# When plain jobs split their weights, and how much selection runs beside the recurrence, in a fp32 hybrid block on one Trainium2 core

## The chip, the cores and the metric

The kernel runs on one core of a Trainium2 chip. The engines are named as the profile names them: PE (TensorE, matrix products; PEld is its loading of the stationary operand), DVE (VectorE), ACT (ScalarE), POOL (GpSimd) and SP (SyncE, here only the queue that starts the transfers). The metric is the device time of one execution in microseconds (us).

## What is computed

The reference is one layer of a streaming block over 512 tokens of width 2048, all in fp32. After an RMS norm, one wide projection gives the inputs of two mixers. Branch A is a gated linear recurrence with 8 heads of 128 (here called the recurrence). Branch B is attention in which a small indexer with 16 heads scores all visible keys and each query keeps its 128 best (here called the selection). Both are gated, projected, merged and projected back.

```python
h = rmsnorm(x, norm_w)
(a_q, a_f, a_i, a_g, c_q, c_kv, k_idx, w_idx, b_g, m_a, m_b) = split(h @ w_in)
q, f, v = silu(a_q) / sqrt(128), lb + (1 - lb) * sigmoid(a_f), a_i
state = exp(sum log f) * state + decayed(1 - f).T @ v      # per chunk of 64
y_a = rmsnorm(q * decay @ state + causal(q, 1 - f) @ v) * silu(a_g)
score = sum_h relu(q_idx[h] @ k_idx.T) * w_idx[h]           # 16 heads
top_val, top_idx = top_k(score, 128)                        # the selection
y_b = softmax(q @ k[top_idx] + t5_bias) @ v[top_idx] * silu(b_g)
x = x + (sigmoid(m_a) * (y_a @ w_pa) + sigmoid(m_b) * (y_b @ w_pb)) @ w_out
return rmsnorm(x, final_norm_w)
```

## The kernel before, in words

Each fp32 product is made of three products of rounded halves: an operand is split into a high part (`wh`, a rounded copy made by ACT, line 90) and a low part (`wl`, the difference, made by DVE, line 91), and `mm3` issues high*high, high*low and low*high (lines 94, 95, 96).

The program is a list of jobs, run in order; each engine works through its own queue in the order in which the program was written. **Plain jobs** are `feat_job` (a tile of features by 512 tokens; the names `cq`, `kx`, `hf`, `hq`, `aq` are its outputs), `ai_job` (the recurrence's values) and `ukv_job`. A plain job takes its weights in chunks of 1024 numbers per partition (512 for the one-tile job of `kx`). **Pair jobs** take 7 products in place of 8 on blocks, with their own preparation in `pair_unit`; the change leaves them as they are.

The way of a chunk: `load` (line 147, queue of SP) fetches it into one of two buffers `wr`; the split reads `wr` and writes one of three pairs `wh`/`wl`; PE reads them. `prep(i)` issues the splits up to chunk i+2, and `load_ahead` the loads for up to two chunks beyond the last one split. A load has to wait until the low part of the chunk two before it has been taken from the same buffer.

Beside the jobs run **lanes**: generators that each do one step whenever a job calls `pump()`, in the order hgrn, top, att, norm, misc, t5. A plain job pumps twice or so in a chunk: `ai_job` after every second of its four k-blocks, a job with two tiles after each tile, the one-tile job after the chunk. The lane `hgrn` (`hgrn_gen`) does the recurrence of two heads in 8 levels. At a level, PE makes a burst of small products (`hl<-hq,hk`, line 99), and then DVE multiplies decay factors into `hq` and `hk` (lines 785, 792, 794; `tot`, line 803, is the running factor), and copies what the level masks (`hnear`, line 816). The next burst reads the new `hq` and `hk`; after the last level PE transposes `hk` (`hkt`, line 834). The lane `norm` has, in the same stretch, products of a vector with a row (`nt`, line 604) that ACT rounds (`ckh`, line 605). The lane `misc` has `pair_gen`: per step sums of x (`sv`, lines 1080 to 1087) and their split (`s`).

The lane `top` (`top_gen`) does the selection: 3 blocks of 16 iterations, each a `MAX8` and a `MATCH_REPLACE8` over the scores `M` (lines 684, 685), and at a block's end one line 687. It paces itself: at each pump its credit grows by 2.7 minus `R.load`, a number that `hgrn_gen` sets at each of its steps, and each iteration costs 0.4 + 0.27(b+1). When the job `uqkv(0)` begins (the first queries of the attention), `drain("top")` issues what is left of the selection at once.

Near the end stands **the merge**: eight jobs of two tiles and two chunks that multiply by `w_pb`. `pb_evac` empties each tile's sum times its gate (`mg<-acc,mg`, line 1365) and adds the other mixer's (line 1366). Behind the second tile a generator `merge_pair` joins the lane `misc`. At the next pumps it takes differences of the two tiles on DVE (`hv`, lines 1339 to 1342) and rounds the tiles on ACT (`mh` and `m21h`, lines 1343 to 1345); then it takes the low parts on DVE (`ml` and `m21l`, lines 1348 to 1350) and rounds and splits the sums (`so`, lines 1347 and 1354). One pump later `m21h` and `m21l` are stored to DRAM (`m_d`, line 1352, queue of SP). There is one buffer for `m21h` and one for `m21l`, so that the rounding for the next two tiles waits until the store has landed. In SP's queue the store stands behind the loads of two chunks, and ahead of the loads of the next gates (line 1300). The output job (`pp`), a pair job, follows; its chunks are split by `prep` as well (lines 164 to 173: `sv`, `bh`, `bl`, `wh`, `wl`), and the first of them within the last of the eight jobs.

The order of the jobs around the change: `cq` in two halves with `kx` between them, `ckv`, the pair jobs of the gates, eight jobs for the indexer, then ai(3) and ai(2), f and q of pair 0, ai(1), f and q of pair 1, `uqkv(0)`, a gate job, and the rest of the attention and of the merge. Beside them run the recurrences of the pairs 3, 2, 0 and 1, in this order.

Of the kernel before, what the change touches and what calls it, by code (L numbers as in the profile page):

```python
# [68 lines left out]
def hybrid_block(ctx, tc, x, norm_w, w_in, lb_table, gnorm_a, q_norm_w, kv_norm_w, w_uq,  # L69
# [19 lines left out]
    def split(hi, lo, src):  # L89
        A.activation(hi, src, AF.Copy)  # L90
        V.tensor_tensor(lo, src, hi.bitcast(F32), op=OP.subtract)  # L91
# [43 lines left out]
    R = SimpleNamespace(load=0.0)  # L135
# [3 lines left out]
    raws, halves = {}, {}  # L139
# [10 lines left out]
    def load_ahead():  # L150
        while issued[0] < min(issued[1] + 2, len(specs)):
            load(issued[0])
            issued[0] += 1

    def weight_places(at):
        return [wpool.tile([128, WCAP + 64], FR, name=name)[:, at:at + WCAP] for name in ("wh", "wl")]
# [19 lines left out]
    def prep(i):  # L176
        while issued[1] < min(i + 3, len(specs)):
            j = issued[1]
            if specs[j][3:4] == ("pair",) and not hasattr(R, "g"):
                if j > i + 1 and lanes["norm"]:  # L180
                    break
                open_pairs()
            load_ahead()
            _, kc, n = specs[j][:3]
            t = raws.pop(j)
            if specs[j][3:4] == ("pair",):
                halves[j] = pair_sums(t, 0 if specs[j][4] else R.at)
                issued[1] += 1
                continue
            if len(specs[j]) > 3 and isinstance(specs[j][3], str):  # L190
                both = R.s2.tile([128, 2, WCAP], FR, name="wk", tag=specs[j][3])
                hi, lo = both[:, 0, :], both[:, 1, :]
            else:
                hi, lo = weight_places(*specs[j][3:] or (0,))
            split(hi[:, :kc * n], lo[:, :kc * n], t[:, :kc * n])
            halves[j] = tuple(a[:, :kc * n].rearrange("p (k n) -> p k n", k=kc) for a in (hi, lo))
            issued[1] += 1

    lanes = {name: deque() for name in ("hgrn", "top", "att", "norm", "misc", "t5")}

    late = [[], []]
# [6 lines left out]
    def pump():  # L208
        load_ahead()
        flush()  # L210
        for lane in lanes.values():
            while lane:
                try:
                    next(lane[0])
                    break
                except StopIteration:
                    lane.popleft()
# [10 lines left out]
    def feat_job(src, col, ntile, nk, kc, rhs, evac, before=None, width=T, after=None, place=0,  # L228
                 often=False):
        at = len(specs)  # L230
        n = ntile * 128
        for k in range(0, nk, kc):
            specs.append(([(0, n, src[k * 128:(k + kc) * 128, col:col + n])], kc, n, place))

        def run():
            if before:
                before()
            ps = [mmp.tile([128, T], F32, name="acc")[:, 0:width] for _ in range(ntile)]
            for i in range(nk // kc):
                prep(at + i)  # L240
                wh, wl = halves.pop(at + i)
                for c in range(ntile):
                    for k in range(kc):
                        kk = i * kc + k
                        rh, rl = rhs(kk)
                        s = slice(c * 128, c * 128 + 128)
                        mm3(ps[c], wh[:, k, s], wl[:, k, s], rh, rl, kk == 0, kk == nk - 1)
                        if often and k == 1:
                            pump()
                    if kk == nk - 1:  # L250
                        evac(c, ps[c])
                    if ntile < 4 or c % 2:
                        pump()
                if after and i in after:
                    after[i]()

        jobs.append(run)
# [437 lines left out]
    def ai_job(p):  # L695
        at = len(specs)
        c0 = 2048 + p * 256
        for k in range(0, NK, 4):
            specs.append(([(0, 256, w_in[k * 128:(k + 4) * 128, c0:c0 + 256])], 4, 256, MOVED))

        def run():
            ps = [mmp.tile([128, T], F32, name="acc") for _ in range(2)]
            for i in range(4):
                prep(at + i)
                wh, wl = halves.pop(at + i)
                for k in range(4):
                    kk = i * 4 + k
                    rh, rl = x_rhs(kk)
                    for t in range(4):
                        s = slice(t * 128, t * 128 + 128)  # L710
                        mm3(ps[t // 2][:, (t % 2) * 256:(t % 2) * 256 + 256], rh[:, s], rl[:, s],
                            wh[:, k, :], wl[:, k, :], kk == 0 and t % 2 == 0, kk == NK - 1)
                    if k % 2 == 1:
                        pump()
            v = hg[p, "v"] = R.v.tile([128, 4, 256], F32, name="hv", bufs=2)
            for i in range(2):
                A.activation(v[:, 2 * i:2 * i + 2, :], ps[i].rearrange("p (t n) -> p t n", t=2), AF.Copy)

        jobs.append(run)
# [43 lines left out]
    def hgrn_gen(p):  # L763
# [4 lines left out]
        near = R.h.tile([128, 8, 32], F32, name="hnear")  # L768
        G.memset(near, 0.0)
        qf, kf, tot = (a.rearrange("p c t -> p (c t)") for a in (q, k, f))  # L770
        R.load = 1.3
        yield

        def scores(l, ps):
# [29 lines left out]
            return nt  # L804

        for l in range(8):
            R.load = (1.7, 2.5, 2.1, 1.8, 1.8, 1.7, 1.3, 1.3)[l]
            if l:
                tot = total(l - 1)
            if l == 4:  # L810
                A.activation(S, zero[:, :, None].to_broadcast([128, 8, 128]), AF.Copy)
            ps = bank("hl")
            scores(l, ps)
            decay(l)
            if l < 6:
                V.copy_predicated(near, R.levels[:, l:l + 1, :].to_broadcast([128, 8, 32]),
                                  ps[:, 0:256].rearrange("p (n t) -> p n t", n=8))
            else:
                m = 1 << (l - 1)
                for h in range(0, 128, 2 * m):  # L820
                    A.activation(S[h:h + m, :, h + m:h + 2 * m],
                                 ps[h:h + m, 0:8 * m].rearrange("p (n t) -> p n t", n=8), AF.Copy)
            if l == 6:
                for h in range(0, 128, 32):
                    A.activation(S[h:h + 32, :, h:h + 32], near[h:h + 32], AF.Copy)
            yield
# [79 lines left out]
    def ukv_job(p):  # L906
        at = len(specs)
        specs.append(([(0, 512, w_ukv[0:256, p * 512:(p + 1) * 512])], 2, 512))

        def run():  # L910
            drain("att")
            prep(at)
            wh, wl = halves.pop(at)
            kt = at_[p, "k"] = [R.a.tile([128, 2, T], FR, name=f"ak{i}") for i in range(2)]
            v = at_[p, "v"] = [R.a.tile([128, 4, 256], FR, name=f"av{i}") for i in range(2)]
            for c in range(2):
                ps = mmp.tile([128, T], F32, name="acc")
                s = slice(c * 256, c * 256 + 128)
                for k in range(2):
                    mm3(ps, wh[:, k, s], wl[:, k, s], R.ckh[:, k, :], R.ckl[:, k, :], k == 0, k == 1)  # L920
                split(kt[0][:, c, :], kt[1][:, c, :], ps)
            pump()
            for t2 in range(2):
                ps = mmp.tile([128, T], F32, name="acc")
                for k in range(2):
                    for t in range(2):
                        s = slice((t2 * 2 + t) * 128, (t2 * 2 + t + 1) * 128)
                        r = [w[:, k, :].rearrange("p (c a d) -> p c a d", c=2, a=2)[:, :, 1, :]
                             for w in (wh, wl)]
                        o = ps[:, t * 256:(t + 1) * 256].rearrange("p (c d) -> p c d", c=2)  # L930
                        mm3(o, R.ckh[:, k, s], R.ckl[:, k, s], r[0], r[1], k == 0 and t == 0, k == 1)
                split(*(a[:, t2 * 2:t2 * 2 + 2, :] for a in v), ps.rearrange("p (t n) -> p t n", t=2))
            lanes["att"].append(att_gen(p))
            pump()

        jobs.append(run)

    def att_bias(h):
# [125 lines left out]
    def open_pairs():  # L1064
        drain("norm")
        drain("misc")
        flush()
        flush()
        leave("norms")
        R.g = enter("pairs")  # L1070
        R.g.tile([128, STILL], F32, name="gap")
        R.sv, R.at = 2, STILL
# [513 lines left out]
```

## Time and profile before

| | us |
|---|---|
| runs shown, median (lowest to highest of 3) | 1358.65 (1358.5 to 1359.09) |
| the profiled execution, its time | 1359.18 |
| its span, from the first instruction to the last | 1357.4 |
| PE busy | 1345.9 |
| weight loads of PE busy | 1249.3 |
| DVE busy | 1074.5 |
| ACT busy | 668.6 |

The profiled execution took 0.53 us longer than the median, and 1.8 us of it lie outside its span. A row of the timeline gives the start of an instruction (us from the span's start), its duration, engine, line, operation, output and inputs, and in brackets the idle time of the engine ahead of it, with what ended it. Matmuls overlap, and their ends are modelled, so that the distance between two starts says more than their durations.

### The profile page before, as it was taken

To read this page: it belongs to the slowest core of one execution; us is meant where nothing else is said; L and a number is where in the kernel's file an instruction comes from. 1 tells how busy PE (TensorE), PEld (TensorE's weight loads), DVE (VectorE), ACT (ScalarE), POOL (GpSimd) and SP (SyncE) were. 2 spreads that over 40 slices of the span, in tenths; PEclk is the share of its full clock that TensorE was granted. 3 is DMA by queue.
4 is the path that set the end of the run, shared out by engine and by line. 5 is a ranking of instruction groups with operands and counts; after the bars stand their busy time and mean duration, and the time that the engine had idled before them with its cause. 6 is when DMAs were issued, how large, how long until landed. Compare 5 with 4: busy or idle time off the path is not lost.

```text
span 1357.4 us, 26813 instructions
## 1 busy us (share of the span) xinstructions
PE 1345.9 (99%) x10954; PEld 1249.3 (92%) x10954; DVE 1074.5 (79%) x1750; ACT 668.6 (49%) x1068; POOL 27.4 (2%) x47
## 2 busy tenths in 40 slices
PE   9999999999999999999999999999999999999997
PEld 8889999999999999999999798888888888899996
DVE  7878889988898888877778888675556658899856
ACT  7556454545554444446744444646434334444444
POOL 0000000000000000000000000020101100000000
PEclk9999999999999999999999999999999999999999
DMA  6244345544454444545234432434856556643563
GB/s 224 72 131 139 98 151 156 171 141 141 125 156 140 117 133 140 156 140 191 68 115 135 131 117 73 140 118 160 290 167 204 181 186 210 210 144 121 169 236 140
DMA packets 145166, 204.80 MB, mean 151 GB/s; under 512 B 10585, under 2 KB 87058, under 8 KB 144914
## 3 DMA queue, kind: packets, MB, share of 16 engines
q1 hardware_dynamic: 144754, 202.82, 47.6%
q8 instruction: 86, 1.41, 0.4%
q14 instruction: 38, 0.31, 0.1%
q10 hardware_dynamic: 288, 0.26, 0.1%
HBM read 167.89 MB, written 35.15 MB: 150 GB/s over the span
## 4 chain that ended last, share of the span: by engine, by line
PE 95%; DVE 2%; ACT 1%; DMA 0%; issue 0%; SPq 0%; DVEq 0%
PE pp L94 15%; PE pp L95 15%; PE pp L96 15%; PE acc L94 14%; PE acc L96 13%; PE acc L95 13%; PE acc L99 2%; PE hl L99 1%; PE ho L99 1%; PE sc L94 1%; PE sc L95 1%; PE sc L96 1%; DMA x<-in_x_dram 0%; DVE wl L91 0%; PE hp L99 0%
## 5 line engine op out<-in xcount | busy, mean ns | idle before, releaser
L169 ACT ACTIVATE bh<-wr 128x768 fp32r<-128x768 f32 x128 | 108.2, 845 | 210.1 <-issue 94.5
L171 ACT ACTIVATE wh<-sv 128x512 fp32r<-128x512 f32 x256 | 152.9, 624 | 91.2 <-DVE sv L164 68.2
L94 PE MATMUL pp<-s,wh 128*128 128x256 f32 x624 | 172.3, 276 | 0.0
L95 PE MATMUL pp<-s,wh 128*128 128x256 f32 x624 | 172.3, 276 | 0.0
L96 PE MATMUL pp<-s,wl 128*128 128x256 f32 x624 | 172.3, 276 | 0.0
L91 DVE TENSOR_TENSOR wl<-wr,wh 128x1024 fp32r<-128x1024 f32 (+1 forms) x102 | 122.9, 1205 | 53.2 <-ACT wh L90 53.1
L173 DVE TENSOR_TENSOR wl<-sv,wh 128x1024 fp32r<-128x1024 f32 x128 | 156.4, 1222 | 5.6
L90 ACT ACTIVATE wh<-wr 128x1024 fp32r<-128x1024 f32 (+1 forms) x102 | 106.0, 1039 | 99.5 <-PE acc L95 58.3
L172 DVE TENSOR_TENSOR bl<-wr,bh 128x768 fp32r<-128x768 f32 x128 | 122.2, 955 | 40.4 <-ACT bh L169 40.1
L94 PE MATMUL acc<-xh,wh 128*128 128x512 f32 x304 | 121.5, 400 | 0.0
L96 PE MATMUL acc<-xh,wl 128*128 128x512 f32 x304 | 118.6, 390 | 0.0
L95 PE MATMUL acc<-xl,wh 128*128 128x512 f32 x304 | 118.5, 390 | 0.0
L95 PEld LDWEIGHTS pp<-s,wh 128*128 128x128 f32 x624 | 117.2, 188 | 0.0
L94 PEld LDWEIGHTS pp<-s,wh 128*128 128x128 f32 x624 | 117.1, 188 | 0.0
L96 PEld LDWEIGHTS pp<-s,wl 128*128 128x128 f32 x624 | 117.1, 188 | 0.0
L94 PE MATMUL pp<-xh,bh 128*128 128x256 f32 x416 | 114.9, 276 | 0.0
L96 PE MATMUL pp<-xh,bl 128*128 128x256 f32 x416 | 114.9, 276 | 0.0
L95 PE MATMUL pp<-xl,bh 128*128 128x256 f32 x416 | 114.9, 276 | 0.0
L94 PE MATMUL acc<-yh,wh 128*128 128x512 f32 x256 | 100.2, 391 | 0.0
L96 PE MATMUL acc<-yh,wl 128*128 128x512 f32 x256 | 99.8, 390 | 0.0
L95 PE MATMUL acc<-yl,wh 128*128 128x512 f32 x256 | 99.7, 390 | 0.0
L164 DVE TENSOR_TENSOR sv<-wr 128x512 f32<-128x512 f32 x128 | 87.7, 685 | 13.3 <-DMA wr<-in_w_in_dram 9.0
(395 smaller groups left out, 3648.6 us busy)
## 6 DMA issues: line engine op xcount, KB each, us to landing
wr<-in_w_in_dram SPq DMA_DIRECT2D x136, 512.0 KB, 3.7
wr<-in_w_out_dram SPq DMA_DIRECT2D x32, 512.0 KB, 3.7
mg<-gate_d SPq DMA_DIRECT2D x48, 256.0 KB, 4.6
gate_d<-c SPq DMA_DIRECT2D x44, 256.0 KB, 5.4
wr<-in_w_in_dram SPq DMA_DIRECT2D x36, 256.0 KB, 2.9
wr<-in_w_pa_dram SPq DMA_DIRECT2D x16, 512.0 KB, 6.1
wr<-in_w_pb_dram SPq DMA_DIRECT2D x16, 512.0 KB, 4.1
x<-in_x_dram SPq DMA_DIRECT2D x8, 512.0 KB, 4.1
```

The costliest lines, as they stand in the source:

```text
L90: A.activation(hi, src, AF.Copy)
L91: V.tensor_tensor(lo, src, hi.bitcast(F32), op=OP.subtract)
L94: PE.matmul(ps, lh, rh, start=first, stop=False, skip_group_check=True)
L95: PE.matmul(ps, lh, rl, start=False, stop=False, skip_group_check=True)
L96: PE.matmul(ps, ll, rh, start=False, stop=last, skip_group_check=True)
L99: PE.matmul(ps, l, r, start=first, stop=last, skip_group_check=True)
L164: V.tensor_tensor(sv[:, 0:2, :], b[:, 1:3, :], b[:, 0:1, :].to_broadcast([128, 2, 256]), op=OP.add)
L169: A.activation(bh, b[:, 1:4, :], AF.Copy)
L171: A.activation(vh[:, i:i + 2, :], sv[:, i:i + 2, :], AF.Copy)
L172: V.tensor_tensor(bl, b[:, 1:4, :], bh.bitcast(F32), op=OP.subtract)
L173: V.tensor_tensor(vl, sv, vh.bitcast(F32), op=OP.subtract)
```

## The change

Before, a plain job called `prep` as the first thing in a chunk, so that the split of the chunk after next was issued ahead of everything else in the chunk. Now a chunk begins with `take`, which only fetches the halves that are there already (and splits only where they are missing), and `prep` is called behind each pump of the chunk, where the lanes have just issued their steps. Behind the second pump it finds nothing left to do. Besides, `R.load` is higher in the recurrence's levels, so that the selection gets less credit there. The products that PE makes, their order on PE, and the number of instructions on every engine stay the same; on DVE, ACT and SP the order changes.

```diff
+    def take(i):
+        if i not in halves:
+            prep(i)
+        return halves.pop(i)
...
     def feat_job(...):
...
             for i in range(nk // kc):
-                prep(at + i)
-                wh, wl = halves.pop(at + i)
+                wh, wl = take(at + i)
...
                         if often and k == 1:
                             pump()
+                            prep(at + i)
                     if kk == nk - 1:
                         evac(c, ps[c])
                     if ntile < 4 or c % 2:
                         pump()
+                        prep(at + i)
...
     def ai_job(p):
...
             for i in range(4):
-                prep(at + i)
-                wh, wl = halves.pop(at + i)
+                wh, wl = take(at + i)
...
                     if k % 2 == 1:
                         pump()
+                        prep(at + i)
...
     def hgrn_gen(p):
...
-        R.load = 1.3
+        R.load = 2.4
...
         for l in range(8):
-            R.load = (1.7, 2.5, 2.1, 1.8, 1.8, 1.7, 1.3, 1.3)[l]
+            R.load = (2.0, 2.5, 2.5, 2.2, 2.1, 2.0, 1.5, 1.5)[l]
...
     def ukv_job(p):
...
-            prep(at)
-            wh, wl = halves.pop(at)
+            wh, wl = take(at)
...
             pump()
+            prep(at)
```

Place 1, DVE in the job ai(2), while the recurrence of pair 3 goes through its levels 6 and 7 (`tot`, `hq`, `hk` are one level's decay, `nt` and `ckl` steps of the lane norm, `M` the selection's scores, `wl` the low part of a chunk's weights). Before:

```order
L604 SCALAR_TENSOR_TENSOR nt<-ckv,cols,rr 128x512
L803 TENSOR_TENSOR tot_8718<-tot_8650 128x32
L792 TENSOR_TENSOR hq<-hq,tot_8718 128x16x32
L794 TENSOR_TENSOR hk<-hk,tot_8718 128x16x32
L607 TENSOR_TENSOR ckl<-nt,ckh 128x512
L91 TENSOR_TENSOR wl<-wr,wh 128x1024
L803 TENSOR_TENSOR tot_8781<-tot_8718 128x16
L792 TENSOR_TENSOR hq<-hq,tot_8781 128x8x64
L794 TENSOR_TENSOR hk<-hk,tot_8781 128x8x64
L673 MEMSET M 128x128
L675 MEMSET M 64x64 x4
```

The same place now (most of these lines of the file are 6 higher than before):

```order
L610 SCALAR_TENSOR_TENSOR nt<-ckv,cols,rr 128x512
L91 TENSOR_TENSOR wl<-wr,wh 128x1024
L809 TENSOR_TENSOR tot_8718<-tot_8644 128x32
L798 TENSOR_TENSOR hq<-hq,tot_8718 128x16x32
L800 TENSOR_TENSOR hk<-hk,tot_8718 128x16x32
L613 TENSOR_TENSOR ckl<-nt,ckh 128x512
L809 TENSOR_TENSOR tot_8775<-tot_8718 128x16
L798 TENSOR_TENSOR hq<-hq,tot_8775 128x8x64
L800 TENSOR_TENSOR hk<-hk,tot_8775 128x8x64
L679 MEMSET M 128x128
L681 MEMSET M 64x64 x4
L91 TENSOR_TENSOR wl<-wr,wh 128x1024
```

The split that stood ahead of the decay of level 7 now stands behind it, and the split of the chunk before it stands between `nt` and the decay of level 6.

Place 2, DVE from the end of the job for q of pair 1 into `uqkv(0)`, where the recurrence of pair 1 begins (`hq<-acc` and `aq<-acc` empty the sums of the two jobs, line 785 is the decay of level 0, lines 792 and 794 that of level 1). Before:

```order
L91 TENSOR_TENSOR wl<-wr,wh 128x1024 x2
L758 SCALAR_TENSOR_TENSOR hq<-acc,hq 128x512 x2
L91 TENSOR_TENSOR wl<-wr,wh 128x1024
L903 SCALAR_TENSOR_TENSOR aq_10721<-acc,aq_10720 128x512
L785 TENSOR_TENSOR hq<-hq,hf 128x1024
L816 COPY_PREDICATED hnear<-levels,hl 128x256
L903 SCALAR_TENSOR_TENSOR aq_10721<-acc,aq_10720 128x512
L792 TENSOR_TENSOR hq<-hq,hf 128x512
L794 TENSOR_TENSOR hk<-hk,hf 128x512
```

The same place now, with lines 690, 691 and 693 for the selection's:

```order
L764 SCALAR_TENSOR_TENSOR hq<-acc,hq 128x512
L690 MAX m_10692<-M 128x8
L691 MATCH_REPLACE M<-m_10692,M 128x512
L690 MAX m_10695<-M 128x8
L691 MATCH_REPLACE M<-m_10695,M 128x512
L690 MAX m_10698<-M 128x8
L691 MATCH_REPLACE M<-m_10698,M 128x512
L693 TENSOR_SCALAR M<-M 128x512
L909 SCALAR_TENSOR_TENSOR aq_10717<-acc,aq_10716 128x512
L791 TENSOR_TENSOR hq<-hq,hf 128x1024
L822 COPY_PREDICATED hnear<-levels,hl 128x256
L91 TENSOR_TENSOR wl<-wr,wh 128x1024
```

The last three iterations of the selection and its closing line, which before had been issued earlier, now stand ahead of `aq` and of the decay of level 0, and the split has moved from ahead of them to behind them.

Place 3, DVE in a job of `w_pb`, from the differences of one pair of tiles to the first step of the next (`mg<-acc,mg` empties a tile's sum, `so` belongs to the pair's sums). Before:

```order
L1348 TENSOR_TENSOR ml_13500<-mg,mh_13499 128x256
L1349 TENSOR_TENSOR ml_13500<-mg,mh_13499 128x512
L1350 TENSOR_TENSOR m21l<-mg,m21h 128x256
L91 TENSOR_TENSOR wl<-wr,wh 128x1024
L1365 TENSOR_TENSOR mg<-acc,mg 128x512
L1366 TENSOR_TENSOR mg<-mg 128x512
L1354 TENSOR_TENSOR so_13503<-hv,so_13503 128x1024
L1365 TENSOR_TENSOR mg<-acc,mg 128x512
L1366 TENSOR_TENSOR mg<-mg 128x512
```

The same place now:

```order
L91 TENSOR_TENSOR wl<-wr,wh 128x1024
L1354 TENSOR_TENSOR ml_13500<-mg,mh_13499 128x256
L1355 TENSOR_TENSOR ml_13500<-mg,mh_13499 128x512
L1356 TENSOR_TENSOR m21l<-mg,m21h 128x256
L1371 TENSOR_TENSOR mg<-acc,mg 128x512
L1372 TENSOR_TENSOR mg<-mg 128x512
L1360 TENSOR_TENSOR so_13503<-hv,so_13503 128x1024
L91 TENSOR_TENSOR wl<-wr,wh 128x1024
L1371 TENSOR_TENSOR mg<-acc,mg 128x512
L1372 TENSOR_TENSOR mg<-mg 128x512
```

Of the job's two splits one now stands ahead of the differences of the pair, and the other between the two tiles' sums, behind `so`. On ACT, in the same job, the roundings stood like this before:

```order
L1343 ACTIVATE mh_13499<-mg 128x256
L1344 ACTIVATE mh_13499<-mg 128x512
L1345 ACTIVATE m21h<-mg 128x256
L1347 ACTIVATE so_13503<-hv 128x1024
L90 ACTIVATE wh<-wr 128x1024
```

And they stand like this now:

```order
L1349 ACTIVATE mh_13499<-mg 128x256
L1350 ACTIVATE mh_13499<-mg 128x512
L1351 ACTIVATE m21h<-mg 128x256
L90 ACTIVATE wh<-wr 128x1024
L1353 ACTIVATE so_13503<-hv 128x1024
```

A rounding of weights that stood behind `so` now stands directly behind `m21h`. On the queue of SP nothing is moved here: two loads of weights, the stores of `m21h` and `m21l`, and four loads of gates follow each other in every job, before and now.

## The prediction

> **What bounds the kernel now.** I read the page first: span, busy times, then the shares of the path that ended last.
>
> ```profile
> span 1357.4 us, 26813 instructions
> ...
> PE 1345.9 (99%) x10954; PEld 1249.3 (92%) x10954; DVE 1074.5 (79%) x1750; ACT 668.6 (49%) x1068; POOL 27.4 (2%) x47
> ...
> PE 95%; DVE 2%; ACT 1%; DMA 0%; issue 0%; SPq 0%; DVEq 0%
> ```
>
> PE is the bound, 95% of the path. Its matmuls keep their number and their order, so the change can only move PE's waits: those that it takes away, and new ones that it makes where DVE, ACT or SP come later than PE. The second view is therefore the waits of PE; columns are the idle time in us, how often, and the longest.
>
> ```profile
> PE hl L99 <- DVE hk L794: 0.7, 2, 0.4
> PE hkt L834 <- issue: 0.7, 1, 0.7
> ```
>
> These three are waits for a decay of the recurrence that stood behind a split. 1.4 us in all is what moving splits can win here. What it can lose has no such bound, so the third view is the timeline of DVE, ACT and SP at each place where the order changes.
>
> **The waits that go.** All three decays now stand ahead of the split that delayed them: **-1.4**.
>
> **ai(2): what is late next.** The split moves behind `nt`, and its rounding on ACT now stands behind `ckh`, which waits for `nt`. So the next decay waits for a chain of both engines.
>
> ```profile
> 691.42 0.55 DVE L91 TENSOR_TENSOR tll<-tl,tlh 8x384 fp32r<-8x384 f32 x1 [1.42 <-ACT tlh L90]
> 692.37 1.22 DVE L91 TENSOR_TENSOR wl<-wr,wh 128x1024 fp32r<-128x1024 f32 x1 [0.40 <-ACT wh L90]
> 693.51 0.42 DVE L803 TENSOR_TENSOR tot<-tot 128x256 f32<-128x256 f32 x1
> 694.64 0.68 DVE L794 TENSOR_TENSOR hk<-hk,tot 128x512 f32<-128x512 f32 x1
> 695.58 0.75 DVE L604 SCALAR_TENSOR_TENSOR nt<-ckv,cols,rr 128x512 f32<-128x512 f32 x1
> 696.24 0.28 DVE L803 TENSOR_TENSOR tot<-tot 128x128 f32<-128x128 f32 x1
> 697.24 0.68 DVE L794 TENSOR_TENSOR hk<-hk,tot 128x512 f32<-128x512 f32 x1
> ...
> 696.36 0.63 ACT L605 ACTIVATE ckh<-nt 128x512 fp32r<-128x512 f32 x1 [4.02 <-DVE nt L604]
> ...
> 695.47 0.75 PE L99 MATMUL hl<-hq,hk 128*32 128x32 f32 x64 [0.36 <-DVE hk L794]
> ...
> 699.10 0.76 PE L99 MATMUL hl<-hq,hk 128*32 128x32 f32 x64
> ```
>
> From the start of `nt` to the next `tot` it takes 0.66 now (695.58 to 696.24). With the split between them it is 0.78 to `ckh` (696.36), 0.55 of `ckh` (0.63 less the 0.1 by which neighbours on ACT overlap), 1.06 for `wh`, 1.14 for `wl` (692.37 to 693.51): 3.5, or 2.9 more. Against that stands slack: `hk` ends at 697.92, PE takes it 0.15 later (695.32 to 695.47), and wants it at 699.10, so 1.0; and DVE comes earlier, since `tot` can follow `tll` directly (691.97 in place of 693.51, 1.5), while PE is 0.4 earlier itself. 2.9 - 1.0 - 1.1 leaves 0.8, and two levels on the same chain stands again, with a slack that is as small. I take 0.7 for each, **+1.4**; the ends are 0 (ACT serves the split before `ckh`) and 1.8.
>
> **uqkv(0): the selection.** With more `R.load` the selection gets fewer steps, and its last three iterations with line 687 are drained when `uqkv(0)` begins. They are queued on DVE ahead of `aq` and of the decay of level 0, for which PE's second burst waits.
>
> ```profile
> 858.38 0.69 DVE L684 MAX8 m<-M 128x8 f32<-128x512 f32 x1
> ...
> 859.89 0.43 DVE L687 TENSOR_SCALAR M<-M 128x512 f32<-128x512 f32 x1
> 860.23 0.74 DVE L883 SCALAR_TENSOR_TENSOR hk<-ho,cols,hk 128x512 f32<-128x512 f32 x1
> ...
> 874.72 0.69 DVE L758 SCALAR_TENSOR_TENSOR hq<-acc,hq 128x512 f32<-128x512 f32 x1 [2.02 <-ACT hq L757]
> ...
> 878.09 1.22 DVE L785 TENSOR_TENSOR hq<-hq,hf 128x1024 f32<-128x1024 f32 x1
> ...
> 880.36 0.76 PE L99 MATMUL hl<-hq,hk 128*32 128x32 f32 x64
> ```
>
> An iteration takes 1.51 (858.38 to 859.89), line 687 0.34 (to 860.23), so 3 x 1.51 + 0.34 = 4.9. They begin at 875.3, behind `hq`, and end at 880.2; then `aq` 0.6 and the decay 1.22, to 882.0, and PE at 882.2 in place of 880.36: +1.8. Behind it the order puts a split of 1.14 ahead of the decay of level 3, which before stood behind it; DVE is still behind there, and I take half of it, +0.6 (between 0 and 1.1). **+2.4.**
>
> **The merge.** Here PE waits for nothing now, and the new order closes a ring. The store of `m21h` stands in SP's queue behind the load of a chunk, which waits for a split to free its buffer. That split now stands behind the emptying of the first tile (lines 1365, 1366) and `so`. And the next `m21h` has to wait for the store, since there is one buffer; `wh` is queued right behind it on ACT.
>
> ```profile
> 1170.38 0.40 ACT L1345 ACTIVATE m21h<-mg 128x256 fp32r<-128x256 f32 x1
> 1173.60 1.06 ACT L90 ACTIVATE wh<-wr 128x1024 fp32r<-128x1024 f32 x1
> 1183.60 0.40 ACT L1345 ACTIVATE m21h<-mg 128x256 fp32r<-128x256 f32 x1
> ...
> 1165.67 0.69 DVE L1365 TENSOR_TENSOR mg<-acc,mg 128x512 f32<-128x512 f32 x1 [0.63 <-PE acc L96]
> 1167.00 1.22 DVE L1354 TENSOR_TENSOR so<-hv,so 128x1024 fp32r<-128x1024 f32 x1
> 1172.32 0.42 DVE L1348 TENSOR_TENSOR ml<-mg,mh 128x256 fp32r<-128x256 f32 x1
> 1173.26 0.42 DVE L1350 TENSOR_TENSOR m21l<-mg,m21h 128x256 fp32r<-128x256 f32 x1
> 1174.69 1.23 DVE L91 TENSOR_TENSOR wl<-wr,wh 128x1024 fp32r<-128x1024 f32 x1 [1.01 <-ACT wh L90]
> 1176.55 0.69 DVE L1365 TENSOR_TENSOR mg<-acc,mg 128x512 f32<-128x512 f32 x1 [0.63 <-PE acc L96]
> 1180.60 0.68 DVE L164 TENSOR_TENSOR sv<-wr 128x512 f32<-128x512 f32 x1
> 1184.12 0.42 DVE L1339 TENSOR_TENSOR hv<-mg 128x256 f32<-128x256 f32 x1
> 1192.85 0.68 DVE L1365 TENSOR_TENSOR mg<-acc,mg 128x512 f32<-128x512 f32 x1
> ...
> 1165.50 0.50 SPq L1352 DMA_DIRECT2D m_d<-m21h  x1
> 1176.38 0.46 SPq L1352 DMA_DIRECT2D m_d<-m21h  x1
> ...
> 1194.19 0.28 PE L94 MATMUL pp<-wh,mh 128*128 128x256 f32 x1
> ```
>
> A round now: `m21h` 0.3 (0.40 less the overlap), `wh` 1.06, `wl` 1.14, the low parts 1.28 (1172.32 to 1173.26, and 0.34), the first tile 1.33 (1165.67 to 1167.00), `so` 1.14, the second `wl` 1.23, then 0.46 until the store is issued (1175.92 to 1176.38): 7.95, and the store's landing. PE's round is 10.88 (1165.67 to 1176.55). So the landing decides, and no row has it. From above it is bounded by 4.9 (1165.50 to the next `m21h` at 1170.38, which waits for it and shows no wait); below by the shortest landing in the list of DMA issues, a store's 2.4; a load of its size and the stores of gates take 4.3 (columns: the queue, how often, KB each, median us from issue to landing):
>
> ```profile
> bh<-bh_d SPq DMA_DIRECT2D x8, 128.0 KB, 4.3
> ...
> gate_d<-mg SPq DMA_DIRECT2D x16, 256.0 KB, 4.3
> ...
> out_dram<-o SPq DMA_DIRECT2D x7, 192.0 KB, 2.4
> ```
>
> I take 4.3, at which the row of its size and that of a store between other transfers both stand. The round is then 12.25, 1.37 longer than PE's. [...]
>
> Lateness against PE: in the second job the store is issued 1.33 + 1.14 + 1.23 + 0.46 = 4.2 behind the first tile, by the rows above at 1169.83, and lands at 1174.1, so `m21h` is 3.75 late against 1170.38. Four rounds of the same kind add 4 x 1.37 = 5.5. The next `m21h` stands 13.22 behind (1170.38 to 1183.60), so a round of 12.25 gives 1.0 back: 8.2. From there to the emptying of the last tile it is 9.25 now (1183.60 to 1192.85). In the changed order it is 0.3, some 1.9 for the roundings of a pair chunk (1792 numbers, `wh` has 1024 in 1.06), 1.14, 1.28, 1.33, 1.14, and the pair split 3.52 (1180.60 to 1184.12), which now stands between the two tiles: 10.6, 1.35 more. The emptying comes 9.5 late. Of that 0.5 is slack (1193.53 + 0.15 to 1194.19), and PE waits **+9.0**, in pieces from the sixth job on, most of it at the first products of the output job.
>
> **Sum.** -1.4 + 1.4 + 2.4 + 9.0 = +11.4. The profiled execution took 1359.18, so 1370.6; it lies 0.53 above the median of the runs shown, so **1370.0**. The other moved splits I cost at nothing, since a chunk is split two chunks before PE takes it, and the groups of waits hold none of PE for `wh` or `wl`; in the first jobs, where chunks are small, a few tenths may be lost.
>
> **The rivals.** *The store lands early.* At 2.4 to 2.9 the round stays within 10.88, PE is never late in the merge, and the +9.0 goes to 0: 1361.0, not slower by what can be told. [...] For it speaks `out_dram` at 2.4; against it `gate_d` at 4.3, and that the store is issued right behind a load of 512 KB and ahead of four of gates. It decides at a landing of 2.9. Chance 0.09.
>
> *The store lands late.* In the changed order its burst is denser: the four loads of gates follow without a pause. At the upper bound of 4.9 a round is 12.85, and the six rounds add 6 x 0.6 = 3.6: 1373.6. Nothing in the trace shows it; chance 0.12.
>
> *PE has room.* [...] If moved waits fill a room on PE, only the gains count and more than they: under 1355.9. The path with 95% PE speaks against it; 0.02.
>
> **How the numbers follow.** My forecast has 0.77. Its own range is 1366 to 1373: landing 4.0 to 4.6 (6 x 0.3 = 1.8 each way), ai(2) 0 to 1.8, the selection 1.8 to 2.9. The range of 1365.5 to 1373.6 holds nearly all of it and about half of the late store. This measurement can tell about 0.2%, 2.7 us, so that faster is under 1355.9 and slower over 1361.4: the forecast and the late store make slower 0.89, the early store same 0.09, room on PE faster 0.02.
>
> **What would show it.** The groups of waits would have PE waiting for `wh`, `wl` and `mg` in the merge, ACT's `m21h` with idle time ended by the DMA `m_d` in each job, and 12.2 between two `m21h`. At `uqkv(0)` the second burst would come 1.8 late behind three iterations; in ai(2) the waits for `hk` would move to the next levels, about 0.7 each. A store that lands under 2.9, or an `m21h` that doesn't wait for it, makes the prediction wrong.

## The result, and the profile after

| | us |
|---|---|
| after, median of 4 runs (lowest to highest) | 1374.19 (1373.71 to 1375.01) |
| before, 4 runs in turn with them | 1358.58 (1358.44 to 1359.09) |
| ratio, with its 95% interval | 1.0115 (1.0097 to 1.0132) |
| the profiled execution of after, its time and its span | 1375.01 and 1373.2 |

The change makes the kernel 15.6 us slower. The forecast was 11.4 slower, and its range ended at 1373.6: the sign and the main mechanism (the merge) were right, the size was too small, and 3.65 us came from two places that the forecast had at nothing.

The page of after answers to that of before: the same counts of instructions on PE, DVE and ACT, and PE's share of the path gone from 95% to 89%.

```profile
span 1373.2 us, 26787 instructions
...
PE 1348.8 (98%) x10954; PEld 1249.4 (91%) x10954; DVE 1076.6 (78%) x1750; ACT 664.9 (48%) x1068; POOL 26.5 (2%) x47
...
PE 89%; DVE 4%; DMA 2%; ACT 2%; issue 1%; SPq 1%; POOL 0%; DVEq 0%; ACTq 0%; POOLq 0%
```

The waits of PE (idle us in all, how often, the longest) name the places. Of these rows the same view of before had only the one for `hk`, with 0.7 in two waits.

```profile
PE pp L94 <- DVE mg L1371: 4.6, 2, 4.3
PE hl L99 <- DVE hk L800: 1.8, 3, 0.7
PE tA L1002 <- DVE P L991: 1.7, 2, 1.4
PE hl L99 <- DVE hq L791: 1.6, 1, 1.6
PE acc L94 <- ACT wh L90: 1.6, 2, 0.9
...
PE acc L96 <- DVE wl L91: 1.3, 3, 0.5
```

Since PE issues the same products in the same order, the two traces can be laid over each other, matmul by matmul. The table gives by how much a matmul of after starts later than the same one of before; its differences say where the 15.65 us of the last matmul come from.

| up to (us in the span of before) | late by | added | what stands there | my term |
|---|---|---|---|---|
| 694 | 0.42 | +0.4 | loads of x at the start, other in every run | 0 |
| 870 | -0.07 | -1.7, +1.4, -0.2 | three waits gone (0.43, 0.83, 0.43), two new (0.69, 0.73), small ones | -1.4, +1.4 |
| 950 | 1.81 | +1.9 | the selection ahead of level 0 | +2.4 |
| 1078 | 3.96 | +2.15 | the softmax of the attention | none |
| 1194.25 | 14.87 | +10.9 | the merge | +9.0 |
| 1198 | 16.35 | +1.5 | the matmuls right behind the longest wait | none |
| 1349.9, the end | 15.65 | -0.7 | 0.6 of it in every traced kernel of this study, so a matter of the one trace of before | 0 |

One name in the text above has to be corrected. What it calls ai(2) is for the most part ai(3): the bursts at 695.47, 699.10 and 706.29 lie in ai(3), and only the decay of the last level and `hkt` at 711.05 at the beginning of ai(2). The steps and their rows are not touched by it.

**The new waits of ai(3).** On the timeline of after, `nt`, the split, the next `tot`; ACT's `ckh` and `wh`; and PE's burst:

```profile
694.48 0.75 DVE L610 SCALAR_TENSOR_TENSOR nt<-ckv,cols,rr 128x512 f32<-128x512 f32 x1
696.88 1.23 DVE L91 TENSOR_TENSOR wl<-wr,wh 128x1024 fp32r<-128x1024 f32 x1 [1.65 <-ACT wh L90]
698.02 0.28 DVE L809 TENSOR_TENSOR tot<-tot 128x128 f32<-128x128 f32 x1
...
695.26 0.63 ACT L611 ACTIVATE ckh<-nt 128x512 fp32r<-128x512 f32 x1 [3.34 <-DVE nt L610]
695.80 1.05 ACT L90 ACTIVATE wh<-wr 128x1024 fp32r<-128x1024 f32 x1
...
699.76 0.76 PE L99 MATMUL hl<-hq,hk 128*32 128x32 f32 x64 [0.62 <-DVE hk L800]
```

From `nt` to `tot` it takes 3.54 (694.48 to 698.02) where it took 0.66: the chain over both engines of which the prediction spoke, at 3.5. DVE itself idles 1.65 of it, since the split that it is to make next waits for ACT.

**The selection.** The three iterations and line 693 stand where the order put them, and PE's burst behind them:

```profile
875.25 0.69 DVE L690 MAX8 m<-M 128x8 f32<-128x512 f32 x1
...
879.79 0.43 DVE L693 TENSOR_SCALAR M<-M 128x512 f32<-128x512 f32 x1
880.14 0.68 DVE L909 SCALAR_TENSOR_TENSOR aq<-acc,aq 128x512 fp32r<-128x512 f32 x1
...
882.01 0.76 PE L99 MATMUL hl<-hq,hk 128*32 128x32 f32 x64 [1.61 <-DVE hq L791]
```

They begin at 875.25 and end at 880.14 (forecast 875.3 and 880.2), and the burst comes at 882.01 (forecast 882.2).

**The softmax, which the prediction did not see.** `bh` is the bias that POOL adds to the mask (`MB`) before DVE can take the row maxima of the scores. Its load is issued by SP. The timeline of after, SP, POOL, DVE and PE:

```profile
1055.08 7.55 SPq L147 DMA_DIRECT2D wr<-in_w_pa_dram  x2
...
1060.98 1.23 DVE L91 TENSOR_TENSOR wl<-wr,wh 128x1024 fp32r<-128x1024 f32 x1 [0.26 <-ACT wh L90]
...
1063.74 1.68 SPq L946 DMA_DIRECT2D bh<-bh_d  x1
...
1068.44 1.43 POOL L954 TENSOR_TENSOR MB<-M,bh 128x256 f32<-128x256 f32 x2 [37.17 <-DMA bh<-bh_d]
...
1069.20 0.48 DVE L972 CUSTOM_DVE_ANT_0 P<-lA,MB,mx 128x256 f32<-128x256 f32 x1 [3.06 <-POOL MB L954]
...
1076.46 0.30 PE L1002 MATMUL tA<-ident,P 128*128 128x128 f32 x1 [1.38 <-DVE P L991]
```

The same places before:

```profile
1058.42 0.38 SPq L147 DMA_DIRECT2D wr<-in_w_pa_dram  x1
...
1059.92 0.44 SPq L940 DMA_DIRECT2D bh<-bh_d  x1
...
1064.34 1.43 POOL L948 TENSOR_TENSOR MB<-M,bh 128x256 f32<-128x256 f32 x2 [36.02 <-DVE mx L966]
```

In after, SP's queue stands from 1055.08 on in front of the second of two weight loads, which needs the buffer that a split frees. That split is now issued behind the pump of the job for the shared keys and values, and its low part is made at 1060.98 to 1062.21. The load of `bh` is queued behind, and comes 3.8 later (1059.92 to 1063.74) on a PE that is 1.8 late; so `MB` is 2.3 late against PE, DVE waits 3.06 for it, and PE waits for `P`.

**The merge.** ACT's `m21h` now has idle time that the DMA `m_d` ends, in each of the six rounds; here the first, the second and the last, and some of SP's issues:

```profile
1134.45 0.42 ACT L1351 ACTIVATE m21h<-mg 128x256 fp32r<-128x256 f32 x1 [2.65 <-DMA m_d<-m21h]
1147.12 0.42 ACT L1351 ACTIVATE m21h<-mg 128x256 fp32r<-128x256 f32 x1 [3.18 <-DMA m_d<-m21h]
...
1197.58 0.42 ACT L1351 ACTIVATE m21h<-mg 128x256 fp32r<-128x256 f32 x1 [3.00 <-DMA m_d<-m21h]
...
1142.41 0.50 SPq L1358 DMA_DIRECT2D m_d<-m21h  x1
...
1149.78 5.25 SPq L147 DMA_DIRECT2D wr<-in_w_pb_dram  x2
1155.08 0.50 SPq L1358 DMA_DIRECT2D m_d<-m21h  x1
```

From `m21h` to the issue of its store it is 7.96 (1134.45 to 1142.41, and again 1147.12 to 1155.08); the prediction's sum was 7.95. From the issue to the next `m21h`, which waits for the landing, it is 4.71 here, and 4.42, 4.70, 4.97 and 4.54 in the rounds that follow: 4.67 in the mean, where I had taken 4.3. (The store ahead of the first of these waits, issued at 1130.28, took 4.17.) So five rounds take (1197.58 - 1134.45) / 5 = 12.63 each, in place of 12.25, against PE's 10.88.

**Behind the longest wait.** PE's first products of the output job, on the timeline, and then two stretches with their length, the busy time (and count) of PE, weight loads, DVE, ACT and POOL, the granted clock, DMA share and GB/s:

```profile
1208.95 0.39 PE L94 MATMUL pp<-wh,mh 128*128 128x256 f32 x1 [4.34 <-DVE mg L1371]
...
1209.78 0.42 PE L94 MATMUL pp<-bh,mh 128*128 128x256 f32 x1
1209.99 0.41 PE L95 MATMUL pp<-bl,mh 128*128 128x256 f32 x1
```

```profile
1208.00:1213.30 5.30, 4.35 (x24) 4.35 (x25) 5.20 (x9) 2.75 (x6) 0.00 (x0) 0.68 0.92 288
1213.30:1220.00 6.70, 6.70 (x61) 6.70 (x60) 6.60 (x13) 3.33 (x5) 0.00 (x0) 1.00 0.58 200
```

From 1209.78 on the matmuls start 0.21 apart, where before had 0.12, for 3.4 us, and the granted clock of the stretch, which takes in some time ahead of the drop, is 0.68. Sixteen spacings at 0.09 to 0.10 more are the 1.5 us of the table. The wait itself is not all that a wait costs.

### The profile page after: what moved, and what is told of

It is laid out like the page before. It is cut to its first block, busy times and chain, and to the rows that moved or that the text cites. A ratio compares the mean times of both kernels' runs of the same rounds, so it can differ in the third digit from the quotient of the medians.

```text
span 1373.2 us, 26787 instructions
## 1 busy us (share of the span) xinstructions
PE 1348.8 (98%) x10954; PEld 1249.4 (91%) x10954; DVE 1076.6 (78%) x1750; ACT 664.9 (48%) x1068; POOL 26.5 (2%) x47
## 4 chain that ended last, share of the span: by engine, by line
PE 89%; DVE 4%; DMA 2%; ACT 2%; issue 1%; SPq 1%; POOL 0%; DVEq 0%; ACTq 0%; POOLq 0%
PE pp L96 15%; PE pp L94 15%; PE pp L95 15%; PE acc L94 12%; PE acc L96 11%; PE acc L95 11%; PE acc L99 2%; PE hl L99 1%; DMA mg<-gate_d 1%; DVE wl L91 1%; PE ho L99 1%; DMA m_d<-m21h 1%; PE sc L94 1%; PE sc L95 1%; PE sc L96 1%
## 5 line engine op out<-in xcount | busy, mean ns | idle before, releaser
L90 ACT ACTIVATE wh<-wr 128x1024 fp32r<-128x1024 f32 (+1 forms) x102 | 105.4, 1036 | 42.9 <-DMA wr<-in_w_in_dram 14.1
```

## The experiments

The theory after the result: (1) the merge loses by a ring, in which the single buffer of `m21h` waits for a store, the store stands in SP's queue behind a load, and the load waits for a split that was moved; (2) the softmax loses because a load stands in the same queue behind such a load; (3) the selection's pile at 880 is the doing of `R.load` alone; (4) a long wait of PE brings slow matmuls behind it. The rivals: the merge loses because the splits themselves come late for PE, the late softmax is only what the late selection leaves, and the slow matmuls come from what runs beside them (DVE and ACT full, DMA at 0.92) and not from the wait.

Times are medians in us, each beside before in turn on the same chip.

| kernel | time | before | ratio (95%) |
|---|---|---|---|
| two buffers | 1361.90 | 1359.12 | 1.0022 (1.0012 to 1.0031) |
| store ahead of loads | 1361.96 | 1359.12 | 1.0021 (1.0012 to 1.0031) |
| old place in the merge | 1361.94 | 1359.12 | 1.0022 (1.0013 to 1.0032) |
| old place ahead of the softmax | 1372.35 | 1358.88 | 1.0099 (1.0082 to 1.0116) |
| old room in the recurrence | 1373.24 | 1359.12 | 1.0107 (1.0091 to 1.0124) |
| new room alone | 1362.67 | 1358.88 | 1.0027 (1.0016 to 1.0038) |
| three undone | 1358.60 | 1358.83 | 0.9999 (0.9990 to 1.0008) |
| split between the lanes | 1357.65 | 1358.83 | 0.9992 (0.9983 to 1.0001) |

### Three ways to open the ring

The first gives `m21h` and `m21l` a second buffer, in the changed kernel:

```diff
-        last = [R.u.tile([128, 256], FR, name=f"m21{i}") for i in "hl"]
+        last = [R.u.tile([128, 256], FR, name=f"m21{i}", bufs=2) for i in "hl"]
```

> The changed kernel (1374.19), with two buffers in place of one for m21h and m21l, so that a rounding no longer waits for the store before it. Theory (the ring through the store): the round of the merge is no longer 12.6 between two m21h but PE's 10.9; of the 10.8 that PE lost in the merge at most 1 stays (the pair split between the last two tiles), and the stretch at half the granted clock behind the long wait goes with it, 1.5 more: 1362 to 1363.5. Rival (the splits between the tiles make DVE late by themselves, the store is only carried along): DVE's order is the same, so the time stays above 1371.

The second changes what SP has first, from the merge on (`R.m` exists only then): the store, and then the loads.

```diff
     def pump():
-        load_ahead()
-        flush()
+        if hasattr(R, "m"):
+            flush()
+            load_ahead()
+        else:
+            load_ahead()
+            flush()
```

> The changed kernel, where a pump in the merge issues the stores (and what else is due) ahead of the loads of weights, so that the store of m21h stands ahead of the load that waits for the split. One buffer as before. Theory: the store leaves some 4 us earlier, lands before the next rounding asks for it, and the merge loses no more than 1: 1362 to 1364. If the store's landing of 4.7 were the cause by itself, wherever it stands in the queue, the time would stay above 1370.

The third puts the split back to the beginning of the chunk, in the eight jobs of `w_pb` alone:

```diff
+                if early:
+                    prep(at + i)
                 wh, wl = take(at + i)
...
-                        prep(at + i)
+                        if not early:
+                            prep(at + i)
...
-        feat_job(w_pb, j * 128, 2, H, 4, y_rhs("yb"), pb_evac(j))
+        feat_job(w_pb, j * 128, 2, H, 4, y_rhs("yb"), pb_evac(j), early=True)
```

> The changed kernel, with the old place of the split (first thing in a chunk) in the eight jobs of the merge alone. Both theories of the merge expect its whole loss to go, 10.8 and 1.5: 1361.5 to 1362.5, with the waits of PE at uqkv(0) (1.7) and at the softmax (tA, 2.1) left. Against the run with two buffers it gives what the order alone costs without the ring: 0.5 to 1 by the theory, all of it by the rival.

All three give the same time, 1361.90 to 1361.96, which is 2.8 over before in place of 15.6 (for the first two just under the lower end of what was expected). Laid over before, what PE loses between 1090 and 1200 falls from 12.3 to 0.5, 0.3 and nothing, so that about 12 hang on this ring, the slow matmuls behind it included; each of its three links is needed for it. (Most of the rest of the 12.8 is the softmax, which costs 1.4 to 1.5 in these three traces in place of 2.15.) The splits stand as late as in after in the first two, so that the rival (late splits alone) falls. With the store ahead of the loads, `m21h` is back at PE's round of 10.88, and shows no wait; the timeline, ACT's first two:

```profile
1130.33 0.40 ACT L1355 ACTIVATE m21h<-mg 128x256 fp32r<-128x256 f32 x1
1141.21 0.40 ACT L1355 ACTIVATE m21h<-mg 128x256 fp32r<-128x256 f32 x1
```

What the first two keep of the merge's loss is a wait of 0.3 at the matmul of 1194.19, which comes 0.4 later: the pair split that now stands between the last two tiles. The third, which moves it back, has none.

### The old place ahead of the softmax

```diff
     def ukv_job(p):
...
+            prep(at)
             wh, wl = take(at)
```

> The changed kernel with the old place of the split in ukv_job alone. Theory: the load of the next chunk then leaves earlier, and so does bh behind it in SP's queue; POOL's sum MB is ready when the softmax asks for it, and PE's waits for P at tA (2.1) go: 1371.5 to 1372.5. Rival (POOL and DVE slow each other there, whatever arrives when): 1374.

It took 13.5 more than before in place of 15.6, so 2.1 less, and both waits for `P` are gone, with the selection's wait at 880 still there: laid over before, PE comes out of the softmax as late as it went in, 1.18. The rival falls. (The whole time measures the softmax less well, since this trace lost 2.1 to slow matmuls behind the merge in place of 1.5.) SP's issue of `bh` on the timeline:

```profile
1061.10 0.45 SPq L947 DMA_DIRECT2D bh<-bh_d  x1
```

It stands 1.2 behind that of before, as late as PE is there itself (1.2).

### The room for the selection, undone and alone

Undone, in the changed kernel:

```diff
-        R.load = 2.4
+        R.load = 1.3
...
-            R.load = (2.0, 2.5, 2.5, 2.2, 2.1, 2.0, 1.5, 1.5)[l]
+            R.load = (1.7, 2.5, 2.1, 1.8, 1.8, 1.7, 1.3, 1.3)[l]
```

> The changed kernel with the old numbers of R.load. Theory: the three drained iterations at uqkv(0) go, and with them PE's wait of 1.7 there; the merge is untouched: 1372 to 1372.6, and PE's old waits at 808 and 812 stay away only if the moved split alone removed them (else up to 0.6 more). Rival (the selection's lateness is carried through the attention into the merge): several us less than that, under 1370.

Over its own before it is 14.1, 1.5 less than after, and the wait at 880.36 is gone, so that (3) stands. The softmax still costs 2.0 in its trace, though nothing is late ahead of it. The time itself was nearer to after than I had expected; before was 0.5 slower in these runs than in those of after, which is most of the miss.

Alone, the same lines of the diff the other way, put into the kernel before:

> The kernel before with the new numbers of R.load alone. Theory: three iterations and line 687 are drained at uqkv(0) as in the changed kernel, the second burst of PE comes late by about 2 (there is a split ahead of it as well), and the waits at 808 and 812 (0.6) may go: 1359.8 to 1361.2. Rival (room in the recurrence is a gain by itself): under 1358.5.

This was a miss: 3.8 more than before, where the whole selection had cost 1.9 in after. The timeline of PE, and the stretch behind, with the clock as the third number from the end:

```profile
883.14 0.76 PE L99 MATMUL hl<-hq,hk 128*32 128x32 f32 x64 [2.74 <-DVE hq L785]
```

```profile
883.10:888.00 4.90, 4.86 (x75) 3.97 (x76) 4.29 (x7) 0.60 (x1) 0.00 (x0) 0.65 0.32 99
```

The same stretch in after, behind its wait of 1.61:

```profile
882.00:887.00 5.00, 4.99 (x145) 4.14 (x146) 4.76 (x9) 1.84 (x3) 0.00 (x0) 1.00 0.38 110
```

Laid over before, the burst comes 2.8 later, 1.1 more than in after (1.7): the low part of the split, 1.14, which stands ahead of the decay here and behind it there. And with the longer wait the slow matmuls come as well, another 1.5. So at this place the moved split is a gain, of about 2.5 (by 950 PE has lost 4.3 here and 1.9 in after), that hides a part of what the new room costs. The DMA share is 0.32 and ACT is all but idle in the slow stretch, which speaks against the rival of (4).

### A wait made by hand

To tell at which length the slow matmuls begin, extra work on DVE was put into the kernel before, ahead of the emptying of the merge's last tile: N multiplications of `u` by 1, which change no number.

```diff
             g, u = mg.pop(32 + j), mg.pop(16 + j)
+            if j == 15:
+                for _ in range(N):
+                    V.tensor_scalar(u, u, 1.0, None, op0=OP.mult)
             V.tensor_tensor(g, ps, g, op=OP.mult)
```

With N = 8 and N = 19 first:

> The kernel before with 8 extra multiplications by 1 on DVE ahead of the last tile's emptying in the merge. PE should wait about 2 us there. If the granted clock falls only behind a wait over some 3 or 4 us, the matmuls behind it start 0.12 apart as ever and the time is about 2.2 over before; if any wait does it, they start 0.21 apart for some 3 us and it is 3.7 over.

> The same with 19 multiplications. PE should wait about 6 us. If a long wait lowers the granted clock, the matmuls behind it start 0.21 apart for some 3 us, and the time is 6.2 and 1.5 over before; if the stretch in the changed kernel had another cause (the loads behind it, DMA at 92%), they start 0.12 apart and it is 6.2 over.

And then, between the wait of 1.6 behind which nothing was slow and that of N = 8:

> The kernel before with six extra multiplications on VectorE ahead of the emptying of the merge's last job. From the run with eight (a wait of TensorE of 2.96 us) at 0.46 us for each, TensorE's wait at the matmul behind them should be 2.0 us, about the length of the wait at 880.36 in the changed kernel (1.7), behind which nothing was slow. If the clock falls only behind waits nearer to 3 us (theory), the matmuls behind stand at their usual 0.11 to 0.12 us and the end is 1.9 to 2.1 us behind the kernel before; if it falls behind any wait of 2 us, they stand 0.21 apart for about 3 us and the end is 3.3 to 3.6 behind.

> The same with seven multiplications: a wait of 2.5 us. Theory (the fall begins near 2.8 us): 2.4 to 2.6 us behind the kernel before and no slow stretch. Rival (it begins between 1.7 and 2.5 us): a stretch at 0.21 us spacing, 3.8 to 4.1 us behind.

The matmul that waits, and the stretch behind it. N = 6:

```profile
1196.78 0.39 PE L94 MATMUL pp<-wh,mh 128*128 128x256 f32 x1 [1.88 <-DVE mg L1368]
```

```profile
1196.70:1199.20 2.50, 2.42 (x21) 2.43 (x22) 2.40 (x6) 0.83 (x2) 0.00 (x0) 1.00 0.27 105
```

N = 7:

```profile
1196.78 0.39 PE L94 MATMUL pp<-wh,mh 128*128 128x256 f32 x1 [2.35 <-DVE mg L1368]
```

```profile
1196.70:1198.30 1.60, 1.52 (x12) 1.53 (x13) 1.53 (x4) 0.14 (x1) 0.00 (x0) 0.95 0.13 47
1198.30:1201.60 3.30, 3.30 (x18) 3.30 (x17) 3.27 (x7) 2.99 (x6) 0.00 (x0) 0.51 0.18 45
```

N = 8:

```profile
1197.93 0.58 PE L94 MATMUL pp<-wh,mh 128*128 128x256 f32 x1 [2.80 <-DVE mg L1368]
```

N = 19:

```profile
1202.66 0.58 PE L94 MATMUL pp<-wh,mh 128*128 128x256 f32 x1 [7.88 <-DVE mg L1368]
```

```profile
1202.00:1208.00 6.00, 5.34 (x25) 5.34 (x26) 5.86 (x12) 3.13 (x6) 0.00 (x0) 0.50 0.17 42
```

| N | wait of PE | extra behind it | one run | before |
|---|---|---|---|---|
| 6 | 1.88 | none | 1361.02 | 1358.83 |
| 7 | 2.35 | 1.5 | 1362.73 | 1358.83 |
| 8 | 2.80 | 1.4 | 1363.71 | 1358.88 |
| 19 | 7.88 | 2.5 | 1369.51 | 1358.88 |

The waits of N = 8 and N = 19 came out longer than expected (2.80 for about 2, 7.88 for about 6), and so did their times. Between N = 6 and N = 7 there is half a microsecond of wait and the same work beside it, so that the wait and not the other engines brings the slow matmuls. The theory that the drop begins near 2.8 falls with N = 7: at this place a wait of 2.35 was enough, and one of 1.88 was not. The drop is to half the clock, 0.50 to 0.51. Behind 2.35 it comes 1.4 us after PE has resumed (the spacing goes from 0.11 to 0.22 at 1198.15), behind 2.80 it is there with the first matmul (0.54 in 1197.20:1199.00).

The length of a wait is not all that counts, though. Behind the wait of 4.34 in after the granted clock was 0.50 from 1209.71 to 1213.13, and the slow matmuls cost 1.5. With the old place ahead of the softmax the wait at the same matmul, 4.3 as well, cost 2.1. No run shows what else sets the cost.

### All three undone at once

The edits of the store, of the shared keys' job and of the old room together, in the changed kernel:

```diff
+        if hasattr(R, "m"):
+            flush()
+            load_ahead()
...
+        R.load = 1.3
...
+            prep(at)
             wh, wl = take(at)
```

> The changed kernel with three things undone at once: the merge's store issued ahead of the loads, the old place of the split in the shared keys' and values' job ahead of the softmax, the old room in the recurrence's steps. Left of the change are the three removed waits (-1.7) and the two new ones at 699.10 and 706.29 (+1.4), and +0.4 in the merge. Theory (the parts add): from the run with the store first (2.8 us behind the kernel before) less 1.9 for the softmax and less 1.9 for the wait at 880.36, 1.0 us ahead of the kernel before: 1357.6 to 1358.6 us. Rival (the parts hide one another, so that undoing one lets the next come out): 1359.5 to 1361.

1358.60 is the upper end of what the theory gave, 0.2 below before and not to be told from it. The parts add within what these runs can tell, and none comes out in the place of another: the trace has no wait for `P` and none for `hq`, and 0.2 for `mg`. What is left of the change gains three waits and loses two.

### A split between two lanes

The last kernel keeps what gains. The merge's jobs and the shared keys' job have the old place, `R.load` the old numbers, and in ai(3) the split stands between the lane of the recurrence and the lane norm:

```diff
-    def pump():
+    def pump(mid=None):
...
-        for lane in lanes.values():
+        for name, lane in lanes.items():
...
+            if name == "hgrn" and mid is not None:
+                prep(mid)
...
     def ai_job(p):
...
-                        pump()
+                        pump(at + i if p == 3 else None)
                         prep(at + i)
```

> The changed kernel with the old place of the split in the merge's jobs and in the shared keys' and values' job, the old room in the recurrence's steps, and in the gates' job before the third level's end the split put between the recurrence lane's step and the normalisation lane's step, so that the normalisation alone goes on ahead of it. Theory: the two new waits at 699.10 and 706.29 go with the split ahead of the other lane, the three removed waits stay removed: 1.4 to 3 us ahead of the kernel before, 1356.0 to 1357.6 us. Rival (the order of the lanes in that chunk doesn't matter, only their amount): the two waits stay, 1358 to 1359 us.

DVE and PE at the place of the new waits:

```profile
694.12 1.22 DVE L91 TENSOR_TENSOR wl<-wr,wh 128x1024 fp32r<-128x1024 f32 x1
695.25 0.75 DVE L615 SCALAR_TENSOR_TENSOR nt<-ckv,cols,rr 128x512 f32<-128x512 f32 x1
695.92 0.28 DVE L814 TENSOR_TENSOR tot<-tot 128x128 f32<-128x128 f32 x1
...
698.84 0.76 PE L99 MATMUL hl<-hq,hk 128*32 128x32 f32 x64
```

The split no longer waits for `ckh`, `nt` is followed by `tot` after 0.67, and PE's bursts there show no wait. The time is 1357.65, at the upper edge of what the theory gave and below the rival's. That is 1.2 us under before, but the ratio is 0.9992 with an interval that still holds 1: the two waits are gone for certain, a gain of the whole kernel is not shown.

## Why the prediction was right about the merge, and too small

- **The waits that go: -1.4.** Right in kind; laid over each other the traces give 0.43 + 0.83 + 0.43 = 1.7.
- **ai(2), in fact ai(3): +0.7 twice.** Right, 0.69 and 0.73, by the chain that it described (3.54 measured, 3.5 forecast). That the split between the lanes takes both away shows that the place behind `nt` is the cause.
- **The selection: +1.8 and +0.6.** The first part was 1.7. The second was 0.2: PE's wait at the matmul of 891.65 grew from 0.14 to 0.51, and half of that was made good behind it. That the split's new place is a gain there, and the same room costs 3.8 without it, the prediction had not asked.
- **The merge: +9.0.** The mechanism was right in each link, and three experiments show it. The step that failed is a term of the sum: "I take 4.3", the landing. It was 4.67 in the mean of the five rounds, which is 0.37 in each, 1.85 of the 1.9 that the merge took more; the rest of its sum, 7.95, was 7.96. The evidence was the store of gates and a load of the same size, both at 4.3; the late rival's 4.9 was reached in one round (4.97) and not in the mean. Whether the denser burst makes it longer isn't shown, since no row of before has the landing. The early rival falls: no store that `m21h` waited for landed under 4.17.
- **The step that failed outright** is the sentence by which the rest cost nothing: "The other moved splits I cost at nothing, since a chunk is split two chunks before PE takes it". For PE's own weights this held outside the merge. But a split also frees a buffer, the load that waits for it stops SP's queue, and whatever is queued behind comes late: the same reasoning that the prediction used in the merge and did not carry to the other jobs. It cost 2.15 at the softmax in the trace of after (1.4 to 2.0 in the four other traces with that split in its new place and the merge or the room alone undone), and nothing in the run with the old place there.
- **A term that was missing:** slow matmuls behind a long wait, 1.5. The prediction put the most of PE's wait in one place and priced it at its length. A wait of 4.3 at the same matmul cost 2.1 in the run with the old place ahead of the softmax, and no run shows why.
- **Sum.** With the measured terms, -1.7 + 1.4 + 1.9 + 10.9 = 12.5; the two missing ones make 16.1, and the difference to 15.65 is the small waits (-0.2) and the start and the end of the traces, which differ from run to run. The late end of the range was the landing's bound, and with two terms left out it was 0.6 too low.

## What to carry to other kernels

When an instruction is moved that frees a buffer, follow the transfer that waits for the buffer, and then everything that stands behind that transfer in its queue; do it in every job, not only where a ring is seen. A moved step that waits for another engine turns one engine's delay into a chain over both, as right behind `nt` here, where 3.54 us took the place of 0.66. Price a wait of the matrix engine at its length only while it is short: here waits of 2.35 us and more cost 1.4 to 2.5 us on top, and waits of 1.61 and 1.88 us nothing.

## What the runs showed of the hardware

- Behind waits of PE of 2.35 (N = 7), 2.80 (N = 8), 4.34 (after) and 7.88 us (N = 19) matmuls of 128x256 started 0.21 us apart in place of 0.12, and the granted clock was 0.51 in 1198.30:1201.60 at N = 7, 0.50 in 1209.71:1213.13 of after and 0.50 in 1202.00:1208.00 at N = 19. Behind a wait of 2.74 us (the new room alone) it was 0.65 in 883.10:888.00.
- Behind waits of 1.61 (after, 882.00:887.00) and 1.88 us (N = 6, 1196.70:1199.20) the granted clock was 1.00.
- A store of 128 KB on SP's queue, issued right behind a load of 512 KB, took 4.2 to 5.0 us from its issue until the engine that waited for it went on (six rounds of the merge in after).
